# Two layers of a hybrid decoder trunk on one core: q and k blocks set between conv blocks, rotation moved to ScalarE and GpSimd, norm sums and reciprocals moved

## The chip, the cores and the metric

The kernel runs on one core of a Trainium2 chip. The core has TensorE (matmuls, called PE in the profile), VectorE (DVE), ScalarE (ACT), GpSimd (POOL) and SyncE (SP), which here issues the loads. Each engine works through its own queue in program order and waits on semaphores for the others. The metric is the time of one execution in microseconds (us); lower is better.

## What is computed

`reference.py`, cut to the layer (256 tokens, 1024 channels, two layers, 4 retention heads with q and k of 128 and v of 256):

```python
h = rmsnorm(x, norm_mix)
cb, cc, cu, q, k, v, g, ga, gb = split(h @ w_in)
y_conv = (cb * causal_conv3(cc * cu, conv_w)) @ w_conv_out
q, k   = rotary(q, positions) * 128**-0.5, rotary(k, positions)
o      = retention(q, k, v)          # decayed causal scores, then values
o      = (o - mean(o)) * rsqrt(var(o) + eps) * ret_norm     # per head
y_ret  = (silu(g) * o) @ w_ret_out
x = x + (sigmoid(ga) * y_conv + sigmoid(gb) * y_ret) @ w_o
x = x + square(relu(rmsnorm(x, norm_mlp) @ w_up)) @ w_down
# after both layers: rmsnorm(x, norm_final)

def rotary(t):                       # per head, halves of 64
    return concat([t1*cos - t2*sin, t1*sin + t2*cos])
```

## The kernel before

All activations lie with channels on the 128 partitions and the 256 tokens along the row. Every float32 operand of a big matmul is kept as two parts in a reduced float32 form, hi (a rounded copy) and lo (the rest), and three of the four products are taken. `split` (L102) makes the parts: ScalarE casts hi (L103), VectorE subtracts to get lo (L104).

The weights come as 152 blocks of 1 MB, in the order in which they are used: per layer 4 for v (blocks 0 to 3), 28 in the order of `IN_ORDER` (L39), then 4 each for the conv output, the retention output and the output projection, 16 for the MLP up and 16 for down. `window(products)` (L137) handles one block: window i first runs the work booked for it, in between splits both halves of block i+2 (1024 columns each, `parts`), then issues the 32 matmuls of block i, then the load of block i+3, then small products booked for this window. So VectorE splits two blocks ahead of TensorE. There are two buffers for raw weights, three for parts and three for the results of a projection.

Work is booked by hand: `at(n, fn, ph=...)` (L122) puts a step n windows later, at phase -1 or 0 (before the first half's split), 1 (between the halves) or 2 (behind them); `products_at` (L125) books small matmuls. Within a window the steps run in the order in which they were booked, and each engine's queue follows that order. A projection's result is taken in one window later by `collect` (L232): a ScalarE copy of one half and a VectorE add of the other.

In the mixing stage, with windows numbered by their block within the layer:

- The norm's sums over channels are a TensorE product with ones (`norm_total`, L420); in the window after it `factors_begin` (L409) and one more later `factors_end` (L415) make the factors `rr` and `rr2` in twelve VectorE steps. It is booked for window 5 in layer 0 and for window 2 in layer 1. `rotations` (L424, window 10) multiplies the cosine and sine tables by them, q's on VectorE (L425, L426) and k's on GpSimd.
- g takes blocks 4 and 5, conv groups 0 and 1 (cc, cu, cb) 6 to 11, q and k 12 to 15, conv groups 2 and 3 16 to 21, g again 22 and 23, ga 24 to 27, gb 28 to 31.
- `rotate` (L449) takes q or k of two heads: GpSimd multiplies by the cosines (L451), VectorE multiplies the two halves of 64 partitions crosswise by the sines (L453, L454), GpSimd adds (L455); a window later the parts are split.
- The conv (L507 to L530) has GpSimd multiplies at `conv_c`, `conv_u`, `conv_in` and `conv_b`, and four VectorE taps in `conv_in`.
- `scores` (L536) of head h is booked 1 + h windows after block 16; `mix_values` (L549), `gate_values` (L560) and `head_sums` (L571) give per head the values' squares, their split `osq`, and their sums over channels `var_ps`. `head_roots` (L577) makes a square root on ScalarE, a window later a reciprocal on VectorE, two windows later a Newton step (`newton`, L239) and `head_out` (L593), a multiply and a split.

## Time and profile before

| what | before |
|---|---|
| median of 3 runs | 906.25 us (905.71 to 907.66) |
| the profiled execution | 909.5 us, span 907.7 us |
| TensorE busy | 885.3 us, 98% |
| VectorE busy | 709.2 us, 78% |
| ScalarE busy | 512.9 us, 57% |
| GpSimd busy | 258.0 us, 28% |
| granted TensorE clock | 0.998 |

The span runs from the first instruction to the last of the profiled execution; all later rows are of it. The rows of an engine in order of time give start, length, engine, line, operation, result and inputs, shape and count, and in square brackets how long the engine had been idle before and what ended that. Layer 0 reaches to some 458 us, with its mixing stage up to 277, and layer 1 from there on.

### The profile page before, as it was taken

What the parts mean: (1) busy time and instruction counts of PE and PEld (TensorE: products, weight loads), DVE (VectorE), ACT (ScalarE), POOL (GpSimd) and SP (SyncE); (2) the same over time, 40 slices, a digit from 0 to 9 for tenths busy, and PEclk for the clock granted to TensorE, in tenths of its full rate; (3) what the DMA queues carried; (4) which work ended last, traced back from release to release, by engine and by line L of the source; (5) the groups of instructions that cost most, each with busy time, mean ns of one, the idle gap of its engine ahead of it and who ended that gap; (6) DMA issues with size and microseconds to landing.
All of it is one profiled execution on the core that took longest, in us unless ns stands there. A gap on an engine that the chain in (4) does not pass through costs nothing.

```text
span 907.7 us, 12561 instructions
## 1 busy us (share of the span) xinstructions
PE 885.3 (98%) x5026; PEld 764.6 (84%) x5026; DVE 709.2 (78%) x796; ACT 512.9 (57%) x733; POOL 258.0 (28%) x168
## 2 busy tenths in 40 slices
PE   9988999999999999999999999999999999999996
PEld 6867788878888888888888888888888888888896
DVE  5779999999898766555567999999999896664551
ACT  5835455765556777544445543656665577763350
POOL 0646545422112322100010655452211222220110
PEclk9999999999999999999999999999999999999999
DMA  8534454445654555555555444544465455555531
GB/s 285 189 133 170 168 179 164 183 144 182 232 192 180 195 186 186 197 185 187 187 184 193 156 174 152 190 182 142 159 247 181 185 202 186 186 192 185 183 138 46
DMA packets 23818, 163.00 MB, mean 180 GB/s; under 512 B 2768, under 2 KB 3152, under 8 KB 4432
## 3 DMA queue, kind: packets, MB, share of 16 engines
q1 hardware_dynamic: 23184, 161.36, 50.3%
q10 hardware_dynamic: 576, 0.84, 0.3%
q8 instruction: 39, 0.64, 0.3%
q14 instruction: 19, 0.16, 0.0%
HBM read 161.14 MB, written 1.05 MB: 179 GB/s over the span
## 4 chain that ended last, share of the span: by engine, by line
PE 64%; DVE 23%; issue 4%; POOL 3%; DMA 3%; ACT 2%; SPq 0%; DVEq 0%; ACTq 0%; POOLq 0%
PE ps L165 64%; DVE parts L104 14%; DMA raw<-w 3%; DVE sum L236 2%; DVE rot L454 1%; ACT parts L103 1%; DVE acc L518 1%; DVE yc L104 1%; POOL ta L504 0%; POOL red L369 0%; DVE sg L565 0%; DVE sg L498 0%; DVE acc L521 0%; POOL ang L384 0%; DVE sg L236 0%
## 5 line engine op out<-in xcount | busy, mean ns | idle before, releaser
L104 DVE TENSOR_TENSOR parts<-raw,parts 128x1024 fp32r<-128x1024 f32 x305 | 434.4, 1462 | 90.9 <-ACT parts L103 90.2
L103 ACT CAST parts<-raw 128x1024 fp32r<-128x1024 f32 x305 | 305.9, 1050 | 138.1 <-PE ps L165 85.0
L165 PE MATMUL ps<-mix,parts 128*128 128x512 f32 (+1 forms) x1792 | 322.9, 340 | 11.0 <-DVE parts L104 7.5
L165 PEld LDWEIGHTS ps<-mix,parts 128*128 128x128 f32 x1792 | 274.5, 188 | 54.8 <-DVE parts L104 10.0
L165 PE MATMUL ps<-up,parts 128*128 128x512 f32 (+1 forms) x1088 | 182.3, 330 | 0.0
L165 PE MATMUL ps<-mlp,parts 128*128 128x512 f32 (+1 forms) x1024 | 181.6, 340 | 0.0
L165 PEld LDWEIGHTS ps<-up,parts 128*128 128x128 f32 x1088 | 160.6, 189 | 21.1
L165 PEld LDWEIGHTS ps<-mlp,parts 128*128 128x128 f32 x1024 | 157.0, 188 | 23.8
L236 DVE TENSOR_TENSOR sum<-ps,sum 128x512 f32<-128x512 f32 x78 | 53.3, 684 | 45.5 <-ACT sum L235 45.3
L730 POOL TENSOR_TENSOR u<-u,rr2m 128x512 f32<-128x512 f32 x32 | 46.1, 1441 | 131.3 <-ACT u L729 118.3
L235 ACT COPY sum<-ps 128x512 f32<-128x512 f32 x78 | 45.3, 581 | 51.3 <-PE ps L165 51.3
L285 POOL TENSOR_TENSOR mix_sum<-mix_sum,sq 128x512 f32<-128x512 f32 x8 | 12.6, 1574 | 155.7 <-ACT sq L283 155.6
L165 PE MATMUL ps<-yc,parts 128*128 128x512 f32 (+1 forms) x256 | 45.6, 340 | 0.0
L165 PE MATMUL ps<-yr,parts 128*128 128x512 f32 (+1 forms) x256 | 45.5, 340 | 0.0
L165 PE MATMUL ps<-mg,parts 128*128 128x512 f32 (+1 forms) x256 | 45.5, 340 | 0.0
L165 PEld LDWEIGHTS ps<-yr,parts 128*128 128x128 f32 x256 | 39.2, 188 | 6.0
L165 PEld LDWEIGHTS ps<-yc,parts 128*128 128x128 f32 x256 | 39.2, 188 | 6.0
L165 PEld LDWEIGHTS ps<-mg,parts 128*128 128x128 f32 x256 | 39.2, 188 | 6.0
L165 PE MATMUL ps<-parts,mix 128*128 128x512 f32 x180 | 41.8, 392 | 0.0
L165 PEld LDWEIGHTS ps<-parts,mix 128*128 128x128 f32 x180 | 33.6, 188 | 7.4 <-ACT mix L271 0.2
L694 DVE SCALAR_TENSOR_TENSOR px_sb<-ps,px_sb 128x256 f32<-128x256 f32 x60 | 24.0, 421 | 15.6 <-PE ps L165 14.6
L642 POOL TENSOR_TENSOR sum<-sum,rr 128x512 f32<-128x512 f32 x8 | 15.8, 1979 | 59.2 <-DVE sum L236 59.2
(175 smaller groups left out, 668.1 us busy)
## 6 DMA issues: line engine op xcount, KB each, us to landing
raw<-w SPq DMA_DIRECT2D x151, 1024.0 KB, 4.8
raw<-w SPq DMA_DIRECT2D x2, 256.0 KB, 4.4
raw<-w SPq DMA_DIRECT2D x1, 512.0 KB, 5.6
px_sb<-px SPq DMA_DIRECT2D x1, 512.0 KB, 8.3
mask_sb<-mask SPq DMA_DIRECT2D x1, 512.0 KB, 5.7
out<-o SPq DMA_DIRECT2D x2, 256.0 KB, 2.4
out<-o ACTq DMA_DIRECT2D x2, 256.0 KB, 2.4
px_sb<-px SPq DMA_DIRECT2D x1, 256.0 KB, 5.8
```

The source lines that it names most:

```text
L103: nc.scalar.copy(hi, src)
L104: nc.vector.tensor_tensor(out=lo, in0=src, in1=hi.bitcast(F32), op=ALU.subtract)
L165: nc.tensor.matmul(o, lhsT=a, rhs=b, start=start, stop=stop, skip_group_check=True)
L235: nc.scalar.copy(t, ps[:, :, 1, :])
L236: nc.vector.tensor_tensor(out=t, in0=ps[:, :, 0, :], in1=t, op=ALU.add)
L285: nc.gpsimd.tensor_tensor(out=self.sum, in0=self.sum, in1=sq, op=ALU.add)
L454: nc.vector.tensor_tensor(out=w_[64:128], in0=t[0:64], in1=both(sinr[0:64, :]), op=ALU.mult)
L518: nc.vector.scalar_tensor_tensor(out=acc[:, j, 1:], in0=z[:, j, :T - 1], scalar=w1, in1=acc[:, j, 1:], op0=ALU.mult, op1=ALU.add)
L642: nc.gpsimd.tensor_tensor(out=z, in0=z, in1=both(rr2), op=ALU.mult)
L694: nc.vector.scalar_tensor_tensor(out=xk, in0=ps[:, j, half, :], scalar=scale, in1=xk, op0=ALU.mult, op1=ALU.add)
L730: nc.gpsimd.tensor_tensor(out=u, in0=u, in1=both(rr2), op=ALU.mult)
```

## The change

- `IN_ORDER`: of the blocks 9 to 15, q, q, k and k now take 9, 11, 13 and 15, and cc, cu, cb of conv group 1 take 10, 12, 14.
- `rotate`: VectorE's two crosswise multiplies are gone. A window later `rotate_halves` copies the halves crosswise on ScalarE and multiplies the whole by the sines on GpSimd, then adds as before; the split of the parts moves one window on. The sign of the sine table is turned to fit.
- `norm_total` is booked for window 5 in both layers, `rotations` for window 9.
- The reciprocal of the heads comes two windows after the root, between the halves of that window's split; the Newton step and `head_out` come one window later than before, and `head_out`'s multiply moves from VectorE to GpSimd.
- `scores` come one window later; seven small buffers in place of six.

```diff
     [("g", G0), ("g", G0 + 256)]
-    + _conv(0) + _conv(1)
-    + [("q", Q0), ("q", Q0 + 256), ("k", K0), ("k", K0 + 256)]
+    + _conv(0)
+    + [e for qk, c in zip((("q", Q0), ("q", Q0 + 256), ("k", K0)), _conv(1)) for e in (qk, c)]
+    + [("k", K0 + 256)]
     + _conv(2) + _conv(3)
...
-            products_at(5, norm_total)
-        else:
-            products_at(2, norm_total)
-        at(10, rotations)
+        products_at(5, norm_total)
+        at(9, rotations)
...
             nc.gpsimd.tensor_tensor(out=d, in0=t, in1=both(cosr), op=ALU.mult)
-            w_ = t2("rot")
-            nc.vector.tensor_tensor(out=w_[0:64], in0=t[64:128], in1=both(sinr[64:128, :]), op=ALU.mult)
-            nc.vector.tensor_tensor(out=w_[64:128], in0=t[0:64], in1=both(sinr[0:64, :]), op=ALU.mult)
+            at(1, rotate_halves, p, t, sinr)
+
+        def rotate_halves(p, t, sinr):
+            w_, d = t2("rot"), qk[:, 2 * p:2 * p + 2, :]
+            nc.scalar.copy(w_[0:64], t[64:128])
+            nc.scalar.copy(w_[64:128], t[0:64])
+            nc.gpsimd.tensor_tensor(out=w_, in0=w_, in1=both(sinr), op=ALU.mult)
             nc.gpsimd.tensor_tensor(out=d, in0=d, in1=w_, op=ALU.add)
...
-            at(1, lambda: nc.vector.reciprocal(rs, rs))
-            at(2, lambda: newton(rs, t2("rs_a", "rs", 1), rm[:, 1, h, :]))
+            at(2, lambda: nc.vector.reciprocal(rs, rs), ph=1)
+            at(3, lambda: newton(rs, t2("rs_a", "rs", 1), rm[:, 1, h, :]))
             for n in range(2):
-                at(2 + n, head_out, 2 * i + n, rs[:, n, :])
+                at(3 + n, head_out, 2 * i + n, rs[:, n, :])
...
-            nc.vector.tensor_tensor(out=y, in0=y, in1=both(rs), op=ALU.mult)
+            nc.gpsimd.tensor_tensor(out=y, in0=y, in1=both(rs), op=ALU.mult)
             at(1, split, y, *yr.pair(h))
...
-                    products_at(1 + h, scores, h)
+                    products_at(2 + h, scores, h)
...
-    cst[:half, 1], cst[half:, 1] = 2.0, -2.0
+    cst[:half, 1], cst[half:, 1] = -2.0, 2.0
```

The queues show where the steps land. VectorE from the first rotation of layer 0 on, before (`rot` are the crosswise multiplies, `sum` a collect, `parts` the split of a weight block):

```order
L236 TENSOR_TENSOR sum<-ps,sum 128x512
L453 TENSOR_TENSOR rot<-sum,sinq 64x512
L454 TENSOR_TENSOR rot<-sum,sinq 64x512
L104 TENSOR_TENSOR parts<-raw,parts 128x1024 x2
L104 TENSOR_TENSOR q_parts<-qk,q_parts 128x512
L236 TENSOR_TENSOR sum<-ps,sum 128x512
L453 TENSOR_TENSOR rot<-sum,sinq 64x512
```

and now, where the collect of q's second pair is the third `sum`:

```order
L237 TENSOR_TENSOR sum<-ps,sum 128x512
L105 TENSOR_TENSOR parts<-raw,parts 128x1024 x2
L237 TENSOR_TENSOR sum<-ps,sum 128x512
L105 TENSOR_TENSOR parts<-raw,parts 128x1024 x2
L105 TENSOR_TENSOR q_parts<-qk,q_parts 128x512
L237 TENSOR_TENSOR sum<-ps,sum 128x512
```

The multiplies are gone, and a conv block's collect and split stand between two of q.

GpSimd at the same place, before (`qk` is the multiply by the cosines and the final add, `acc` and `sum` are conv steps):

```order
L524 TENSOR_TENSOR acc<-acc,rr 128x512
L529 TENSOR_TENSOR acc<-sum,acc 128x512
L451 TENSOR_TENSOR qk<-sum,cosq 128x512
L455 TENSOR_TENSOR qk<-qk,rot 128x512
L451 TENSOR_TENSOR qk<-sum,cosq 128x512
```

and now:

```order
L527 TENSOR_TENSOR acc<-acc,rr 128x512
L532 TENSOR_TENSOR acc<-sum,acc 128x512
L450 TENSOR_TENSOR qk<-sum,cosq 128x512
L457 TENSOR_TENSOR rot<-rot,sinq 128x512
L458 TENSOR_TENSOR qk<-qk,rot 128x512
L645 TENSOR_TENSOR sum<-sum,rr_138 128x512
L450 TENSOR_TENSOR qk<-sum,cosq 128x512
```

Each rotation has a third GpSimd step, and a conv step follows it.

VectorE at the first pair of heads' reciprocal in layer 0, before (`rm` is the root, `osq` the split of a head's squares, `ta` the collect of ga):

```order
L588 RECIPROCAL rm<-rm 128x512
L565 SCALAR_TENSOR_TENSOR sg<-o_ps,hg,sg 128x256 x2
L236 TENSOR_TENSOR ta<-ps,ta 128x512
L104 TENSOR_TENSOR parts<-raw,parts 128x1024 x2
L241 TENSOR_TENSOR rs_a<-rm 128x512
L242 SCALAR_TENSOR_TENSOR rs_a<-rs_a,rm 128x512
L243 SCALAR_TENSOR_TENSOR rm<-rs_a,rm 128x512
L598 TENSOR_TENSOR sg<-sg,rm 128x512
L104 TENSOR_TENSOR osq<-osq 128x256
```

and now, from the same `sg` step on:

```order
L568 SCALAR_TENSOR_TENSOR sg<-o_ps,hg,sg 128x256 x2
L237 TENSOR_TENSOR ta<-ps,ta 128x512
L105 TENSOR_TENSOR parts<-raw,parts 128x1024 x2
L105 TENSOR_TENSOR osq<-osq 128x256
L237 TENSOR_TENSOR ta<-ps,ta 128x512
L105 TENSOR_TENSOR parts<-raw,parts 128x1024
L591 RECIPROCAL rm<-rm 128x512
L105 TENSOR_TENSOR parts<-raw,parts 128x1024
```

The last `osq` split, which stood behind the reciprocal and the Newton step, now stands ahead of them, and the reciprocal is between two halves of a block's split.

## Rows read from the trace of the kernel before

**Rows 1.** The page's busy time of each engine: us, share of the span, instructions.

```profile
PE 885.3 (98%) x5026; PEld 764.6 (84%) x5026; DVE 709.2 (78%) x796; ACT 512.9 (57%) x733; POOL 258.0 (28%) x168
```

**Rows 2.** Groups of TensorE: count, busy us and mean ns, idle us before and releasers.

```profile
L165 PE MATMUL ps<-mix,parts 128*128 128x512 f32 (+1 forms) x1792 | 322.9, 340 | 11.0 <-DVE parts L104 7.5 <-ACT parts L103 1.2 <-DVE sum L236 1.0
...
L165 PE MATMUL var_ps<-osq,ones 128*128 128x512 f32 x8 | 3.2, 444 | 2.4 <-DVE osq L104 2.4
```

**Rows 3.** TensorE in order of time, layer 0, from block 15 on.

```profile
100.88 5.92 PE L165 MATMUL ps<-mix,parts 128*128 128x256 f32 x32 [0.47 <-DVE parts L104]
107.99 5.92 PE L165 MATMUL ps<-mix,parts 128*128 128x256 f32 x32 [1.20 <-DVE parts L104]
...
121.95 5.59 PE L165 MATMUL ps<-mix,parts 128*128 128x256 f32 x31 [0.44 <-DVE parts L104]
...
192.24 0.50 PE L165 MATMUL var_ps<-osq,ones 128*128 128x512 f32 x1 [1.60 <-DVE osq L104]
```

**Rows 4.** TensorE in order of time, layer 1, from block 4 on.

```profile
480.56 79.29 PE L165 MATMUL ps<-mix,parts 128*128 128x512 f32 x448
...
630.40 0.50 PE L165 MATMUL var_ps<-osq,ones 128*128 128x512 f32 x1 [0.79 <-DVE osq L104]
630.74 17.11 PE L165 MATMUL ps<-mix,parts 128*128 128x512 f32 x96
```

**Rows 5.** VectorE in order of time, layer 1, windows 5 to 18.

```profile
487.97 2.36 DVE L104 TENSOR_TENSOR parts<-raw,parts 128x1024 fp32r<-128x1024 f32 x2 [0.25 <-ACT parts L103]
...
516.54 0.96 DVE L425 TENSOR_TENSOR cosq<-cos_t,rr 128x256 f32<-128x256 f32 x1
...
527.46 0.47 DVE L518 SCALAR_TENSOR_TENSOR acc<-sum,px_sb,acc 128x255 f32<-128x255 f32 x1
...
534.66 0.68 DVE L236 TENSOR_TENSOR sum<-ps,sum 128x512 f32<-128x512 f32 x1
535.37 0.69 DVE L453 TENSOR_TENSOR rot<-sum,sinq 64x512 f32<-64x512 f32 x1
536.07 1.69 DVE L454 TENSOR_TENSOR rot<-sum,sinq 64x512 f32<-64x512 f32 x1
537.79 3.45 DVE L104 TENSOR_TENSOR parts<-raw,parts 128x1024 fp32r<-128x1024 f32 x2
541.17 0.68 DVE L104 TENSOR_TENSOR q_parts<-qk,q_parts 128x512 fp32r<-128x512 f32 x1
541.77 0.68 DVE L236 TENSOR_TENSOR sum<-ps,sum 128x512 f32<-128x512 f32 x1
...
566.56 0.41 DVE L545 TENSOR_TENSOR sc<-sc_ps,mask_sb 128x256 f32<-128x256 f32 x1
```

**Rows 6.** VectorE in order of time, layer 1, windows 6, 7 and 9.

```profile
492.67 0.69 DVE L236 TENSOR_TENSOR sg<-ps,sg 128x512 f32<-128x512 f32 x1 [1.02 <-ACT sg L235]
...
498.33 0.69 DVE L236 TENSOR_TENSOR sum<-ps,sum 128x512 f32<-128x512 f32 x1 [2.35 <-ACT sum L235]
...
512.38 4.24 DVE L104 TENSOR_TENSOR parts<-raw,parts 128x1024 fp32r<-128x1024 f32 x2
```

**Rows 7.** GpSimd in order of time, layer 1: two conv multiplies of one shape.

```profile
499.10 1.31 POOL L642 TENSOR_TENSOR sum<-sum,rr 128x512 f32<-128x512 f32 x1 [33.16 <-DVE sum L236]
...
520.28 2.22 POOL L642 TENSOR_TENSOR sum<-sum,rr 128x512 f32<-128x512 f32 x1 [2.17 <-DVE sum L236]
```

**Rows 8.** VectorE in order of time, layer 1, windows 27 and 28.

```profile
619.24 3.34 DVE L588 RECIPROCAL rm<-rm 128x512 f32<-128x512 f32 x1
...
629.93 0.42 DVE L104 TENSOR_TENSOR osq<-osq 128x256 fp32r<-128x256 f32 x1
...
630.87 3.46 DVE L104 TENSOR_TENSOR parts<-raw,parts 128x1024 fp32r<-128x1024 f32 x2
```

**Rows 9.** VectorE in order of time, layer 0, window 9.

```profile
69.69 1.12 DVE L498 SCALAR_TENSOR_TENSOR sg<-th,sg 128x512 f32<-128x512 f32 x1 [2.21 <-ACT th L497]
```

**Rows 10.** ScalarE in order of time, layer 1: a collect's copy.

```profile
540.72 0.58 ACT L235 COPY sum<-ps 128x512 f32<-128x512 f32 x1
```

More of the change, by code (lines that the diff above doesn't have):

```diff
@@ L75, in trunk_kernel @@
     ones_f = const.tile([P, 1], F32, name="ones_f")
-    idle = tmp.tile([P, 2 * T], BF16, tag="tmp1", bufs=6, name="idle")
+    idle = tmp.tile([P, 2 * T], BF16, tag="tmp1", bufs=7, name="idle")
     cst_sb = const.tile([P, 2], F32, name="cst_sb")
@@ L291, in split_sum @@
         def split_sum(self):
-            self.sums = tuple(tmp.tile([P, T], F32R, tag="tmp1", bufs=6, name=f"{self.name}_{n}") for n in ("sh", "sl"))
+            self.sums = tuple(tmp.tile([P, T], F32R, tag="tmp1", bufs=7, name=f"{self.name}_{n}") for n in ("sh", "sl"))
             split(self.sum[:, 0, :], *self.sums)
@@ L327, in trunk_kernel @@
     nc.scalar.activation(eps2, eps, AF.Square)
-    xs = tmp.tile([P, T], F32, tag="tmp1", bufs=6, name="xs")
+    xs = tmp.tile([P, T], F32, tag="tmp1", bufs=7, name="xs")
     nc.vector.tensor_scalar(out=xs, in0=x[:, 0, :], scalar1=norm.gain[:, 0:1], scalar2=None, op0=ALU.mult)
@@ L362, in late_loads @@
     def late_loads():
-        pos_i = tab["pos"] = tmp.tile([P, T], I32, tag="tmp1", bufs=6, name="pos_i")
+        pos_i = tab["pos"] = tmp.tile([P, T], I32, tag="tmp1", bufs=7, name="pos_i")
         nc.sync.dma_start(out=cst_sb, in_=cst)
@@ L371, in reduce_angles @@
     def reduce_angles():
-        ang, turns, red = (tmp.tile([P, T], F32, tag="tmp1", bufs=6, name=nm) for nm in ("ang", "turns", "red"))
+        ang, turns, red = (tmp.tile([P, T], F32, tag="tmp1", bufs=7, name=nm) for nm in ("ang", "turns", "red"))
         tab.update(ang=ang, turns=turns)
@@ L386, in sines @@
     def sines():
-        half_sin = tab["sh"] = tmp.tile([P, T], F32, tag="tmp1", bufs=6, name="sh")
+        half_sin = tab["sh"] = tmp.tile([P, T], F32, tag="tmp1", bufs=7, name="sh")
         ang, turns = tab["ang"], tab["turns"]
@@ L409, in factors_begin @@
         def factors_begin(norm=norm):
-            rs_m, rs_a = (tmp.tile([P, T], F32, tag="tmp1", bufs=6, name=n) for n in ("rs_m", "rs_a"))
+            rs_m, rs_a = (tmp.tile([P, T], F32, tag="tmp1", bufs=7, name=n) for n in ("rs_m", "rs_a"))
             rsqrt_begin(rr, rs_m, norm.total_ps, 1.0 / D)
@@ L786, in square_last @@
         def square_last(k, ps):
-            sq = tmp.tile([P, T], F32, tag="tmp1", bufs=6, name="sq1")
+            sq = tmp.tile([P, T], F32, tag="tmp1", bufs=7, name="sq1")
             nc.scalar.activation(sq, ps, AF.Square)
```

## The prediction

> **What bounds the kernel now.** I read the page's busy times first, then the groups of TensorE, then each engine in order of time. TensorE is busy for 885.3 of 907.7 us [rows 1], and the change adds no matmul, so all that can be won is idle time of TensorE. The groups put nearly all of it in two places: 11.0 us ahead of the projections on the normed input ("ps<-mix,parts") and 2.4 us ahead of the head sums ("var_ps") [rows 2]. The chain of waits runs through VectorE for most of both mixing stages; that only says that VectorE is there as late as TensorE, and what counts is where TensorE really stood still.
>
> In order of time, layer 1 shows none in its first blocks: fourteen blocks in 79.29 us, 5.66 us a block [rows 4]; that is the floor. In layer 0 TensorE waits for the lo half of a block at 100.88, 107.99, 115.11 (the same length as 107.99) and 121.95: 0.47 + 1.20 + 1.20 + 0.44 = 3.31 us [rows 3]. These are the blocks that VectorE splits while it takes in q, q, k, k. The head sums wait 1.60 us in layer 0 and 0.79 in layer 1 [rows 3, 4]. The other 7.7 us of the 11.0 lie before these, at the start of layer 0.
>
> Why q and k are slow is in the VectorE rows [rows 5]: from one collect to the next 7.11 us (534.66 to 541.77), 1.45 over the floor, four times in a row. The two half multiplies take 0.69 and 1.69 us for the same shape, and the two splits 3.45 us where the plain pair takes 2.36. The second multiply and the splits run while GpSimd runs, and GpSimd's own multiply takes 1.31 us alone but 2.22 beside VectorE [rows 7]. So a GpSimd multiply isn't free to VectorE: it costs it 1.00 to 1.09 us. That decides this change, since it moves work from VectorE to GpSimd.
>
> **The change part by part.** I number the windows of a layer by their block. Rows that follow each other overlap by some 0.08 us, so I count from start to start: split pair 2.28, a 128x512 step 0.60, a 128x256 one 0.34, the four conv taps 1.83, a half multiply 0.70 [rows 5, 8].
>
> *The price of GpSimd.* Windows 10 to 17 of layer 1 take VectorE from 516.54 to 566.56, 50.0 us or 6.25 a window [rows 5]. The VectorE work alone is 8 x 2.28 + 8 x 0.60 + four rotations of 1.5 + 1.83 + two table steps 0.84 + five 128x512 steps 3.0 + two short ones 0.66 = 35.4. GpSimd has 13 full multiplies and two half ones there, 14 in all: (50.0 - 35.4)/14 = 1.05 us each.
>
> *Rotation and order.* Per rotation VectorE loses 1.4 us of multiplies, and gains one more GpSimd multiply, 1.05: only 0.35 us is saved. What the order does is more: the four long windows are apart. VectorE's own work in windows 10 to 17 after the change is 8 x 2.28 + 8 x 0.60 + 1.83 + five steps 3.0 + one short 0.33 = 28.2, and GpSimd has 17 multiplies, 17.9: 46.1 us, 5.76 a window. One by one: 5.1, 6.0, 4.5, 6.0, 7.4, 6.0, 4.9, 6.0. Against 5.66 the lateness runs -0.5, -0.2, -1.3, -0.9, +0.8, +1.2, +0.4, +0.8. If VectorE enters window 10 with no lead, as in layer 0, TensorE stands 1.2 us in place of 3.3: **2.1 us won in layer 0**. The ScalarE copies of 64 rows are two of at most 0.58 us [rows 10], on an engine with 57% busy, behind the cast of a block that isn't due yet: nothing, unless that queue is held (second rival). The changed sign of the sine table costs nothing.
>
> *Factors a window earlier.* The q factors move ahead of window 9's gate step. In layer 0 VectorE is idle there for 2.21 us [rows 9], in which the two could run (0.96 each beside GpSimd [rows 5]); but the gate step waits for a GpSimd multiply that they would slow, so between 1.8 us won and 1 us lost; I take zero, since the multiplies queued on GpSimd there are what the idle waits for.
>
> *Reciprocals.* Before, the 3.34 us reciprocal, the Newton step and a 128x512 multiply stand on VectorE ahead of the split of the last squares ("osq", 629.93), for which the head sums wait [rows 8]. Now the split of the squares comes ahead of the reciprocal, sooner by more than its 3.34 us and so by more than the 1.60 that TensorE waited, and what ends last there is TensorE's own earlier block: **2.4 us won in both layers**. The reciprocal now stands between the halves of a block's split. The next to be late is that second half, but VectorE works there ahead: the split from 630.87 ends at 634.3 [rows 8], and its block starts one block after 630.74 [rows 4], at 636.4, and needs the second half at some 639. That hides 3.3 us; with the cover gone it would be up to 3.3 us for each of four.
>
> *Head outputs to GpSimd.* Eight multiplies of 0.60 leave VectorE and eight of 1.05 on it come: 0.45 x 8 = 3.6 us more for VectorE, four of them a layer. The windows behind (the conv output projection) have only two 128x512 steps and a split, 3.5 us, so it is caught up there: zero.
>
> *Norm sums later in layer 1.* Twelve steps of 128x256 (0.42 each [rows 8], 5.1 us in all) leave windows 3 and 4 for 6 and 7. The first waits for TensorE's column sums behind block 5, which ends at 480.56 + 2 x 5.66 = 491.9, while VectorE has been free since 487.97 + 2.36 = 490.3 [rows 4, 5]: some 2 us, with the value steps and the gate's collect queued behind. It fills idle times of 1.02 and 2.35 us [rows 6] and three of 0.25, 4.1 in all, and the factors (2 x 0.96) come a window sooner. 2.0 + 5.1 - 4.1 + 1.9 is 4.9; some of it lies where the splits ran beside GpSimd, and I take 4.4 us for the start of window 9's split, at 512.38 [rows 6]. Its block is due at 480.56 + 7 x 5.66 = 520.2, and the first half was ready at 514.5: 5.7 us of cover, 1.3 left or, with the heavier GpSimd traffic, about 1.1. The peak of 1.2 then gives **0.1 us lost**.
>
> The sum: 2.1 + 2.4 - 0.1 = 4.4 us. The profiled execution took 909.5 us (span 907.7 and 1.8 around it), which gives 905.1; from the median of 906.25 it is **901.9 us**.
>
> **The rivals.** *GpSimd costs VectorE its whole length (slower).* If each multiply holds VectorE for the 1.31 us that it takes alone [rows 7], 34 multiplies in the two stretches add 0.26 each, 8.8 us: 906.25 - 4.4 + 8.8 = 910.7. It decides from 1.18 us a multiply (no change). For it: each rotation has three in a row now, and layer 1 has no lead left. Against it: two in one window cost (4.24 - 2.36)/2 = 0.94 [rows 6], less than one alone.
>
> The Trainium skill, "SBUF — State Buffer", section "Who interferes with whom", speaks for this rival: a VectorE step with two SBUF inputs and a GpSimd step that reads SBUF share a port, and the one that comes second is blocked until the first has finished. By that rule alone the price is the full 1.31 and the time this rival's; the rows agree that the two exclude each other, but show 1.05 us of the 1.31, and by them the sum stands.
>
> *ScalarE held by GpSimd (same).* ScalarE's q cast, the conv scaling and the yc cast now stand behind GpSimd chains of three, 3 x 2.22 = 6.7 us against a window of 5.66. If windows 14 and 16 each lose 0.75 us in both layers, 3 us come back: 904.9. Against it: two windows together bring GpSimd 8.9 us of 11.3.
>
> *The factors fall into the idle time (faster still).* At 0.94 a multiply the peak of 1.2 goes, 5.7 us won, and with the 1.8 of the factors 7.5: 898.8.
>
> *The wait at the head sums stays*, because the squares' GpSimd sum or its cast is what comes last: 2.4 back, 904.3. In the rows the split starts where the multiply before it ends, so VectorE's order is what held it.
>
> **How the numbers follow.** Forecast 0.55 (900.5, at 0.94 a multiply, to 904.4); factors in the idle time 0.13; head sums stay 0.04; ScalarE held 0.17; GpSimd's whole length 0.11. About 0.2%, 1.8 us, is what a measurement can tell here: faster means under 904.4. Faster 0.55 + 0.13 + 0.04 = 0.72; same 0.17; slower 0.11. The range runs from 898.8 (the best rival) to 907.0 (a price a little over 1.18), with some 0.05 below and 0.12 above.
>
> **What would show it.** Waits of TensorE: the four at q and k at most 1.5 us in sum, "var_ps" none, layer 1 under 0.5 before its head sums. VectorE: windows 10 to 17 in 46 us, split pairs of 3.4 to 4.4, reciprocals between two splits. GpSimd: eight more multiplies at the rotation at 2.2 us, eight at the head outputs. I am wrong if layer 1 shows TensorE waiting for splits between 515 and 560 us, if the split pair beside three multiplies grows past 4.5, or if ScalarE's casts show waits for GpSimd that end after VectorE asks for them.

## The result, and the profile after

| what | before | after |
|---|---|---|
| median | 906.04 us (905.71 to 907.66, 4 runs) | 891.07 us (890.09 to 892.57, 4 runs) |
| ratio, 95% interval | | 0.9833 (0.9814 to 0.9851) |
| the profiled execution | 909.5 us, span 907.7 | 891.4 us, span 889.6 |
| TensorE busy, 5026 matmuls each | 885.3 us | 873.4 us |
| waits ahead of "ps<-mix,parts" and "var_ps" | 11.0 + 2.4 us | 6.7 + 0 us |

Faster, as forecast, but by 15 us where 4.4 were forecast, and outside the range. The page's busy line of after:

```profile
PE 873.4 (98%) x5026; PEld 762.5 (86%) x5026; DVE 705.1 (79%) x772; ACT 524.1 (59%) x749; POOL 294.2 (33%) x184
```

The groups of TensorE in after (count, busy us and mean ns of one, idle us before them and what ended it), beside [rows 2]:

```profile
L166 PE MATMUL ps<-mix,parts 128*128 128x512 f32 (+1 forms) x1792 | 320.5, 339 | 6.7 <-DVE parts L105 3.1 <-DVE sum L237 2.1 <-ACT vt L471 1.5
L166 PE MATMUL ps<-up,parts 128*128 128x512 f32 (+1 forms) x1088 | 179.3, 326 | 0.0
L166 PE MATMUL ps<-mlp,parts 128*128 128x512 f32 (+1 forms) x1024 | 178.4, 336 | 0.0
...
L166 PE MATMUL var_ps<-osq,ones 128*128 128x512 f32 x8 | 2.7, 420 | 0.0
```

and two groups of before that the prediction had not looked at, since nothing waits there:

```profile
L165 PE MATMUL ps<-up,parts 128*128 128x512 f32 (+1 forms) x1088 | 182.3, 330 | 0.0
L165 PE MATMUL ps<-mlp,parts 128*128 128x512 f32 (+1 forms) x1024 | 181.6, 340 | 0.0
```

The span is 18.1 us shorter. Waits of TensorE account for 4.3 + 2.4 = 6.7 us of it. The other 11 to 12 us are TensorE's own busy time: the same matmuls of the same shapes, in stages that the change does not touch and in which TensorE waits for nothing, are 4 ns each shorter. That is the part to be explained.

**The waits.** TensorE in after in order of time (start, length, operation and count; in brackets the idle time ahead and what ended it), both layers:

```profile
35.37 5.92 PE L166 MATMUL ps<-mix,parts 128*128 128x512 f32 x32 [1.51 <-ACT vt L471]
...
60.39 11.14 PE L166 MATMUL ps<-mix,parts 128*128 128x256 f32 x63 [1.72 <-DVE parts L105]
73.67 0.47 PE L166 MATMUL ps<-mix,parts 128*128 128x512 f32 x1 [2.14 <-DVE sum L237]
75.47 46.16 PE L166 MATMUL ps<-mix,parts 128*128 128x256 f32 x255 [1.34 <-DVE parts L105]
...
184.91 0.64 PE L166 MATMUL var_ps<-osq,ones 128*128 128x512 f32 x2
...
479.98 72.42 PE L166 MATMUL ps<-mix,parts 128*128 128x512 f32 x416
...
616.10 0.64 PE L166 MATMUL var_ps<-osq,ones 128*128 128x512 f32 x2
```

From 75.47 on 255 matmuls follow each other with no wait: the four waits at q and k of [rows 3] are gone, and in layer 1 thirteen blocks pass with none, so moving the norm sums and putting more on GpSimd took nothing there. Both second head sums come without the waits of [rows 3, 4]. What is left, 1.51 + 1.72 + 2.14 + 1.34 = 6.7 us, lies in the first twelve blocks of layer 0.

VectorE in after, layer 1: the first and the last row of windows 10 to 17 with the two longest waits between them, the first step of the norm factors, and the second reciprocal's window:

```profile
480.18 0.42 DVE L248 TENSOR_SCALAR rs_m<-mix_st 128x256 f32<-128x256 f32 x1 [1.96 <-PE mix_st L166]
...
508.05 0.68 DVE L501 SCALAR_TENSOR_TENSOR sg<-th,sg 128x512 f32<-128x512 f32 x1
...
525.27 4.09 DVE L105 TENSOR_TENSOR parts<-raw,parts 128x1024 fp32r<-128x1024 f32 x2 [1.16 <-ACT parts L104]
...
542.89 0.69 DVE L105 TENSOR_TENSOR yc<-acc,yc 128x512 fp32r<-128x512 f32 x1 [0.40 <-ACT yc L104]
...
552.22 1.51 DVE L105 TENSOR_TENSOR k_parts<-qk,k_parts 128x256 fp32r<-128x256 f32 x1
...
610.85 0.41 DVE L105 TENSOR_TENSOR osq<-osq 128x256 fp32r<-128x256 f32 x1
...
614.36 3.34 DVE L591 RECIPROCAL rm<-rm 128x512 f32<-128x512 f32 x1
```

From 508.05 to the step that opens window 18, at 552.22, are 44.2 us, 5.52 a window, where 50.0 were in [rows 5] and 46.1 were forecast; 1.9 of them are idle. The last squares are split at 610.85, ahead of the reciprocal at 614.36, and TensorE wants them at 616.10.

**The pace.** The first fourteen blocks behind the norm of the MLP in layer 0, before:

```profile
288.90 79.31 PE L165 MATMUL ps<-mlp,parts 128*128 128x512 f32 x448
```

and after:

```profile
280.25 77.82 PE L166 MATMUL ps<-mlp,parts 128*128 128x512 f32 x448
```

5.66 us a block against 5.56, with no wait in either. The busy time in stretches of 60 us (busy of TensorE with its matmuls, granted clock, DMA share, GB/s), before:

```profile
300.00:360.00 60.00, 60.00 (x342) 1.00 0.54 193
```

and after:

```profile
290.00:350.00 60.00, 60.00 (x349) 1.00 0.57 204
```

The granted clock is 1.00, its 2.4 GHz level, in both; yet TensorE starts 2% more matmuls. The starts of single matmuls show how. In such a stretch a matmul of 512 columns and one of 256 alternate; the distances between starts, in ns, read from the two traces at 320 us, are:

```
before: 120 236 113 233 117 241 | 120 236 113 233 117 241     6 matmuls in 1060 ns, 5.65 us a block of 32
after:  117 230 116 230 117 230 | 116 230 117 230 116 230     6 matmuls in 1040 ns, 5.55 us a block of 32
```

(The second also comes as 113 232 118 231 112 233, in the same 1040 ns.) These are two paces, not a spread: every long stretch of every trace here holds the one or the other until something comes between. That can be little: twice a stretch changed where a single start was 4 ns out of place. I call the two paces slow and fast. Counted over windows of 12 matmuls, before's profile has 3775 matmuls in the slow pace and 342 in the fast one, after's 600 and 3521: some 3180 matmuls at 3.3 ns, 10.5 of the 11.9 us.

### The profile page after: what moved, and what is told of

Its sections match the earlier page's. It is cut to its first block, busy times and chain, and to the rows that moved or that the text cites. A ratio compares the mean times of both kernels' runs of the same rounds, so it can differ in the third digit from the quotient of the medians.

```text
span 889.6 us, 12565 instructions
## 1 busy us (share of the span) xinstructions
PE 873.4 (98%) x5026; PEld 762.5 (86%) x5026; DVE 705.1 (79%) x772; ACT 524.1 (59%) x749; POOL 294.2 (33%) x184
## 3 DMA queue, kind: packets, MB, share of 16 engines
HBM read 161.14 MB, written 1.05 MB: 182 GB/s over the span
## 4 chain that ended last, share of the span: by engine, by line
PE 71%; DVE 17%; DMA 4%; POOL 3%; issue 2%; ACT 2%; SPq 0%; DVEq 0%; ACTq 0%; POOLq 0%
PE ps L166 70%; DVE parts L105 10%; DMA raw<-w 4%; ACT parts L104 1%; DVE sum L237 1%; DVE rm L591 1%; PE o_ps L166 1%; POOL rot L457 1%; POOL qk L450 1%; POOL ta L507 1%; POOL qk L458 0%; DVE acc L521 0%; DVE acc L524 0%; DVE rs_a L242 0%; DVE rs_a L243 0%
## 5 line engine op out<-in xcount | busy, mean ns | idle before, releaser
L166 PE MATMUL ps<-up,parts 128*128 128x512 f32 (+1 forms) x1088 | 179.3, 326 | 0.0
L166 PE MATMUL ps<-mlp,parts 128*128 128x512 f32 (+1 forms) x1024 | 178.4, 336 | 0.0
```

Of the source, the lines that this page charges most:

```text
L166: nc.tensor.matmul(o, lhsT=a, rhs=b, start=start, stop=stop, skip_group_check=True)
```

## The experiments

Two questions: what sets the pace, and which part of the change brings what. The theory was that the phase in which the stream of matmuls is broken and restarts decides (A); the rival, that the pace follows from load elsewhere (VectorE, GpSimd, loads) or from the parts of the change directly (B). Each kernel was timed against the kernel before on its own chip; a ratio has its 95% interval. "Fast" and "slow" with a count are matmuls in the two paces in its profile.

**Reciprocals alone.** The kernel before, with

```diff
-            at(1, lambda: nc.vector.reciprocal(rs, rs))
-            at(2, lambda: newton(rs, t2("rs_a", "rs", 1), rm[:, 1, h, :]))
+            at(2, lambda: nc.vector.reciprocal(rs, rs), ph=1)
+            at(3, lambda: newton(rs, t2("rs_a", "rs", 1), rm[:, 1, h, :]))
...
-                at(2 + n, head_out, 2 * i + n, rs[:, n, :])
+                at(3 + n, head_out, 2 * i + n, rs[:, n, :])
```

> The kernel before with the reciprocals' part of the change alone. Theory A (TensorE's pace is set anew at each restart of its matmul stream and then kept; the change won 11.9 us of its time by that, above all because the head sums no longer wait): the 2.4 us of wait at var_ps go, and behind the second head sums the matmuls come at 173.3 ns on average in place of 176.6, for some 1400 matmuls in layer 0 and 1300 in layer 1: 4.6 + 4.3 + 2.4 = 11 us, about 895. Theory B (the pace belongs to the new block order, the moved rotation or the buffers): 2.4 us, about 903.6, and 176.6 ns throughout.

Measured: 901.33 us against 909.4, ratio 0.9928 (0.9904 to 0.9951). The wait at "var_ps" is 0. Behind the second head sums of both layers the pace is fast for 364 matmuls. It ends at the output projection ("mg"), in layer 1 behind a wait of 0.34 us and in layer 0 behind two starts that come 0.19 us late together; layer 0 then runs slow to its end: 1732 fast, 2357 slow. More than the 2.4 us of the wait, less than if the fast pace had held.

**The change without the reciprocals.** The kernel after, with those lines turned back.

> The changed kernel with the reciprocals where they were before (the head outputs stay on GpSimd). Theory A: waits at var_ps of 1 to 2.4 us come back, and behind them the slow pace of 176.6 ns: 891 + 2 + 9 = about 902. Theory B: the pace stays at 173.3 ns, about 893.

Measured: 895.43 us against 909.4, 0.986 (0.9841 to 0.9879). "var_ps" waits 1.1 us, the pace behind it stays fast for only 117 matmuls and is then mostly slow up to the output projection, in layer 0 up to the MLP, but the MLP of both layers runs fast (3132 fast, 959 slow). So the reciprocals are one way to the fast pace, and not the only one.

**Seven buffers alone.** The kernel before, with `bufs=7` in place of 6 for the small tiles.

> The kernel before with seven small buffers in place of six and nothing else, so that the tiles behind them lie elsewhere in memory. Theory A: no difference, 906.0 within 0.2%, pace 176.6 ns from 193 us on. Theory B in its form that the place of the buffers sets the pace: 173.3 ns and about 894.

Measured: 904.42 us against 909.4, 0.9958 (0.9942 to 0.9974), where no difference was expected. "var_ps" waits 2.0 us, and the pace is mostly slow (1150 fast, 2953 slow), but 822 matmuls of the MLP in layer 1 are fast. The buffer does more than it seems. The rows of VectorE and TensorE in before, early in layer 0:

```profile
49.15 0.43 DVE L241 TENSOR_TENSOR rs_a<-rr 128x256 f32<-128x256 f32 x1 [4.22 <-POOL ang L384]
...
52.56 0.46 PE L165 MATMUL ps<-mix,parts 128*128 128x512 f32 x1 [0.77 <-DVE sg L236]
53.60 5.60 PE L165 MATMUL ps<-mix,parts 128*128 128x256 f32 x31 [0.58 <-DVE parts L104]
60.35 0.49 PE L165 MATMUL ps<-mix,parts 128*128 128x512 f32 x1 [1.16 <-ACT parts L103]
62.57 11.14 PE L165 MATMUL ps<-mix,parts 128*128 128x256 f32 x63 [1.72 <-DVE parts L104]
```

and with seven buffers:

```profile
45.00 0.87 DVE L241 TENSOR_TENSOR rs_a<-rr 128x256 f32<-128x256 f32 x1
...
40.53 17.41 PE L165 MATMUL ps<-mix,parts 128*128 128x512 f32 x97
59.67 11.34 PE L165 MATMUL ps<-mix,parts 128*128 128x256 f32 x63 [1.73 <-DVE parts L104]
```

With six buffers a step of the norm factors waits 4.22 us for GpSimd's work on another small tile, and TensorE then waits 0.77 + 0.58 + 1.16 = 2.5 us for what comes late behind that step; with seven none of this happens, and the block of 62.57 starts 2.9 us sooner. The three waits of TensorE stand in all ten profiles with six buffers and in none of the ten with seven, the changed kernel's among them. The ratio gives 3.8 us; the rest is within what the pace moves between executions.

**A pair of small matmuls that does nothing.** This changes nothing but the place of a break. The kernel before, and behind block 46, 47 or 48 of each layer (early in the MLP), or behind 46 and 47, the column sums of the norm are formed once more: two matmuls of 256 columns into a tile that nobody reads. The norm's own sums behind block 45 are such a pair too.

```diff
+        def idle_pair(norm=norm):
+            o = ps_misc.tile([P, T], F32, tag="misc", name="idle_ps")
+            column_sums(o, *norm.sums)
+
+        products_at(2, idle_pair)          # 2, 3, 4: behind block 46, 47, 48
```

> The kernel before with two more matmuls of 128x256 behind block 46 of each layer (the second MLP block after the norm's sums; ones by operands that are long there, nothing reads the result), which wait for nothing. Theory A, with the phase read from the traces: in the slow pace the starts lie 233, 117, 241, 120, 236, 113 ns apart, over and over, and two small matmuls put in after ...233, 117 or ...241, 120 were followed by the fast pace, after ...236, 113 by the slow one. Block 46 ends after 233, 117: the pace turns to 173.3 ns for some 920 matmuls in layer 0 and 790 in layer 1, 5.7 us won for 0.5 us of added work: about 900.8. Theory B: the 0.5 us are lost, 906.5, and the pace stays.

> As before, but behind block 47, which ends after ...241, 120 ns where the stream is slow. Theory A: that phase was followed by the fast pace, so 173.3 ns for some 890 and 760 matmuls, 5.5 us won less 0.5: ratio 0.9945. Theory B (the pace belongs to the order or the buffers): ratio 1.0005.

> As the kernel with two more matmuls behind block 46, but behind block 48. Theory A (pace set by the phase at which the stream is broken): where the stream before is slow, block 48 ends after ...236, 113 ns, the phase that kept the slow pace in both layers of the kernel before: 176.6 ns stays behind the pair, and 0.5 us are lost, ratio 1.0005. Theory C (any two matmuls put in, wherever, turn the pace): as behind block 46, ratio 0.995.

> The kernel before with the idle pair behind block 46 of each layer, for a second profile. In the first one the norm sums behind block 45 had already turned the slow stream fast, and the pair came into a fast stream. Phase theory (A), now stated by the last distance between starts ahead of the break: behind 235 or 236 ns a slow stream stays slow, behind 232 or 233 and behind 240 or 241 it turns fast, and a fast stream stays fast. So wherever the norm sums (288 us and 723 us) leave the stream slow, block 46 is slow, the pair comes 16 big matmuls later, behind 233, and the 919 and 790 matmuls behind it are fast. Load theory (B): slow on both sides of the pair. Time 903 to 905 us by A, 905 to 910 by B.

> The kernel before with idle pairs behind block 46 and behind block 47. A: a slow stream turns at the first pair at the latest (at the second one if the phase there should be wrong), and a fast one passes both unchanged, so the MLP of both layers is fast in every execution: about 904.4 us as with one pair, 0.2 us more for the second pair in each layer, spread 3 us. B: as the kernel before, 907 us plus 0.9 for the four pairs, spread 7 us.

Measured:

| idle pair behind block | median us | before us | ratio (95%) |
|---|---|---|---|
| 46 | 904.14 (903.33 to 904.58) | 909.4 | 0.9952 (0.9934 to 0.997) |
| 46, second profile | 903.83, one run | 906.97 | |
| 47 | 904.43 (902.67 to 905.05) | 907.22 | 0.9959 (0.9937 to 0.9982) |
| 48 | 909.46 | 907.22 | 1.0011 (0.9989 to 1.0033) |
| 46 and 47 | 904.87 (903.31 to 907.85) | 906.97 | 0.9978 (0.996 to 0.9995) |

One useless pair behind block 46 or 47 makes the kernel 0.4 to 0.5% faster, and 11 runs with it spread over 2.4 us where before's own spread over 7; behind block 48 it does nothing. Both pairs together bring no more than one, and spread over 4.5 us where 3 were expected. The first profile with the pair behind block 46 could not show why: there the norm's sums behind block 45 had just turned the stream fast in both layers, and the pair came into a fast stream. The second profile shows it in layer 1, TensorE in order of time:

```profile
723.57 0.28 PE L165 MATMUL mlp_st<-mlp_sh,ones 128*128 128x256 f32 x1
723.68 0.28 PE L165 MATMUL mlp_st<-mlp_sl,ones 128*128 128x256 f32 x1
723.80 5.81 PE L165 MATMUL ps<-mlp,parts 128*128 128x512 f32 x32
729.45 0.28 PE L165 MATMUL idle_ps<-mlp_sh,ones 128*128 128x256 f32 x1
```

Block 46 takes 729.45 - 723.80 = 5.65 us, the slow pace; behind the pair 790 matmuls follow at the fast one, as expected. Its busy time in stretches ahead of the pair and behind it:

```profile
660.00:720.00 60.00, 59.73 (x342) 1.00 0.58 207
740.00:800.00 60.00, 60.00 (x348) 1.00 0.55 193
```

and with the pair behind block 48:

```profile
660.00:720.00 60.00, 60.00 (x341) 1.00 0.58 211
740.00:800.00 60.00, 60.00 (x342) 1.00 0.53 191
```

The same loads, the same work on all other engines, the same granted clock: rival B falls for the MLP. The pairs behind 46 and 47 turned a slow stream in three places of the profiles, and left it slow in none; the pair behind 48 met two slow streams and left both slow.

The starts give the rule. In the slow pace the distance behind a 512-column matmul runs 233, 241, 236 and again. Over the profiles of all these kernels, wherever two small matmuls come into a running stream (the norms' sums and the idle pairs), what follows goes by the last such distance:

```
last distance ahead of the break     slow stream goes on slow   slow stream goes on fast
235 or 236 ns                                             21                          0
232 or 233 ns                                              0                         19
240 or 241 ns                                              0                         12
(a fast stream goes on fast in 32 of 32)
```

A block has 16 such matmuls, one more than a multiple of three, so each block moves the break on by one place in the cycle: that is why a slow stream that the norm's sums behind block 45 left slow turns behind 46 and behind 47, and not behind 48. What in the chip makes the two paces no run shows.

**The order alone, the rotation alone.** The kernel before with the new `IN_ORDER` and nothing else (the scores stay where they were, unlike what its expectation says), and the kernel before with the new `rotate`:

```diff
-            w_ = t2("rot")
-            nc.vector.tensor_tensor(out=w_[0:64], in0=t[64:128], in1=both(sinr[64:128, :]), op=ALU.mult)
-            nc.vector.tensor_tensor(out=w_[64:128], in0=t[0:64], in1=both(sinr[0:64, :]), op=ALU.mult)
+            at(1, rotate_halves, p, t, sinr)
...
-                    products_at(1 + h, scores, h)
+                    products_at(2 + h, scores, h)
```

> The kernel before with the new order of the blocks alone (q, q, k and k between conv blocks, scores a window later); the rotation stays on VectorE. VectorE has the same work in windows 10 to 17, 50.0 us less 0.9 of score steps that move on. If it is VectorE's sum that makes TensorE wait (my forecast's reading), the waits at q and k stay at 2 to 3.3 us and the time within 1 us; if it is the four long windows in a row, they fall under 1 us. The pace behind the stretch is not changed by either on its own account: the head sums still wait, so mostly slow; where a run starts anew in the other phase, up to 4 us come off.

> The kernel before with the rotation moved to ScalarE and GpSimd and nothing else (scores a window later, as they need it). At my forecast's price of 1.05 us a GpSimd multiply VectorE saves 0.35 us a rotation, 1.4 a layer: the waits at q and k fall from 3.3 to 1.9 us. At the price that the changed kernel's windows 10 to 17 show, (44.2 - 28.2 - 1.9 of waits)/17 = 0.83, it saves 0.6 a rotation, 2.4 a layer: waits of 0.9 us. Ratio 0.997 to 0.9985, and the slow pace stays.

Measured: the order alone 907.75 us against 907.22, 0.9998 (0.9983 to 1.0014); the rotation alone 902.72 against 907.22, 0.9927 (0.9899 to 0.9954), more than was expected of it. With the order alone the group of TensorE waits as before:

```profile
L166 PE MATMUL ps<-mix,parts 128*128 128x512 f32 (+1 forms) x1792 | 324.5, 342 | 10.9 <-DVE parts L105 8.0 <-ACT parts L104 1.1 <-ACT vt L469 0.8
```

and in order of time the waits have only come together:

```profile
85.62 22.87 PE L166 MATMUL ps<-mix,parts 128*128 128x256 f32 x128 [3.09 <-DVE parts L105]
110.32 12.71 PE L166 MATMUL ps<-mix,parts 128*128 128x256 f32 x63 [1.83 <-DVE parts L105]
```

With the rotation alone:

```profile
L165 PE MATMUL ps<-mix,parts 128*128 128x512 f32 (+1 forms) x1792 | 321.0, 339 | 7.4 <-DVE parts L104 4.2 <-ACT parts L103 1.1 <-DVE sum L236 1.1
...
L165 PE MATMUL ps<-mg,parts 128*128 128x512 f32 (+1 forms) x256 | 46.2, 340 | 1.8 <-DVE mg L685 1.4 <-DVE mg L104 0.4
...
L165 PE MATMUL var_ps<-osq,ones 128*128 128x512 f32 x8 | 3.2, 444 | 3.0 <-DVE osq L104 3.0
```

All 7.4 us lie at the start of layer 0, and behind the last of these waits TensorE runs on past q and k:

```profile
83.54 39.00 PE L165 MATMUL ps<-mix,parts 128*128 128x256 f32 x223 [0.57 <-DVE parts L104]
```

The waits at q and k go with the multiplies, not with the order. The wait at the head sums grows to 3.0 us, and one of 1.8 appears at the output projection: TensorE arrives earlier at places where the next thing is late. The three groups together wait 12.2 us, where before's two profiles have 13.4 and 12.8, so alone the rotation mostly moves its waits on, and most of the 0.7% is pace (2941 fast, 1148 slow in this profile). Only with the new reciprocals do the waits at the head sums go as well.

**The change with one part undone.** The kernel after once more, unchanged, and with one part turned back at a time: the head outputs on VectorE, the norm sums of layer 1 at window 2, the rotation on VectorE, the old order, the factors at window 10.

```diff
+            nc.vector.tensor_tensor(out=y, in0=y, in1=both(rs), op=ALU.mult)      # head outputs
...
+        products_at(5 if layer == 0 else 2, norm_total)                           # norm sums
...
+            nc.vector.tensor_tensor(out=w_[0:64], in0=t[64:128], in1=both(sinr[64:128, :]), op=ALU.mult)   # rotation
+            nc.vector.tensor_tensor(out=w_[64:128], in0=t[0:64], in1=both(sinr[0:64, :]), op=ALU.mult)
...
+    + _conv(0) + _conv(1)                                                         # order
+    + [("q", Q0), ("q", Q0 + 256), ("k", K0), ("k", K0 + 256)]
...
+        at(10, rotations)                                                         # factors
```

> The changed kernel, unaltered, beside the three that undo one part of it. Both theories: ratio 0.983 again. Theory A adds: the fast pace of 173.3 ns in the same places (behind the second head sums of both layers and behind the norm's sums), some 3500 of 4200 matmuls.

> The changed kernel with the multiply of the head outputs back on VectorE. My forecast put this part at zero: no wait of TensorE goes or comes, so within 1 us of the changed kernel. Only a small wait elsewhere that breaks the stream in another phase could move it, by up to 3 us a stretch.

> The changed kernel with layer 1's norm sums in window 2 again. My forecast put the move at 0.1 us lost for waits of VectorE. Theory A: in the changed kernel these sums, behind block 5, turned the pace from slow to fast for 375 matmuls; behind block 2 they come before the stream has its 512, 256 beat, so blocks 4 to 17 of layer 1 stay at 176.6 ns, 1.3 to 1.5 us lost: ratio to the changed kernel 1.0015.

> The changed kernel with the rotation's multiplies back on VectorE (order, reciprocals, head outputs, norm sums and factors as changed). By the run with the order alone, VectorE's sum makes TensorE wait: 2 to 3.5 us of waits come back in layer 0 and, with the norm sums' work ahead of them, up to 3 in layer 1; behind the head sums the pace is fast as in the changed kernel: 894 to 898, ratio 0.987 to 0.991.

> The changed kernel with the blocks in the order before (q, q, k, k behind conv group 1), all else as changed. If the order carries the gain at q and k, as my forecast had it, the four long windows in a row are back and 2 us or more of waits with them: ratio 0.983 or more. If the order is idle, as the run with the order alone suggests, the waits stay at 5 to 7 us and the ratio at 0.980.

> The changed kernel with the rotation factors in window 10, as before. My forecast put their move at zero for TensorE. In the changed kernel VectorE spends 3.0 us on two of them in layer 0 before the gate step, while GpSimd has the same port busy, and TensorE then waits 2.1 us for the collect behind and 1.3 for a split: if the factors are what is late, 1 to 2 us of that go, ratio 0.979; if they only fill the wait for the gate's tanh, nothing changes.

| the kernel after, with | median us | ratio to before (95%) | wait at "ps<-mix,parts" | fast, slow |
|---|---|---|---|---|
| nothing undone | 891.2 | 0.9802 (0.9781 to 0.9824) | 5.0 | 2628, 1496 |
| head outputs on VectorE | 890.72 | 0.982 (0.9771 to 0.9868) | 5.7 | 3679, 492 |
| norm sums at window 2 | 892.4 | 0.9818 (0.98 to 0.9837) | 5.2 | 3017, 1121 |
| rotation on VectorE | 898.72 | 0.9887 (0.9867 to 0.9907) | 10.0 | 3316, 759 |
| old order | 892.26 | 0.9819 (0.9788 to 0.9849) | 4.4 | 2285, 1854 |
| factors at window 10 | 891.29 | 0.9822 (0.9791 to 0.9852) | 6.5 | 2396, 1711 |

The first four rows come from one chip, the last two from another (before's medians there: 909.24 and 906.71 us). Unaltered, the kernel gave the same time again, but its fast pace fell short of the 3500 matmuls expected: in this profile the MLP of layer 1 ran slow. In this table the rotation is the only part whose undoing costs something outside the intervals, 7.5 us, and in the profiles 5.0 of waits come back. The reciprocals, turned back further above, gave 0.986, above both ratios of the unaltered kernel (0.9802 and 0.9833). The seventh buffer was not undone by itself. The group of TensorE in that kernel:

```profile
L166 PE MATMUL ps<-mix,parts 128*128 128x512 f32 (+1 forms) x1792 | 324.5, 341 | 10.0 <-DVE parts L105 8.7 <-ACT vt L467 0.6 <-DVE sum L237 0.6
```

The norm sums at window 2 bring 468 slow matmuls in layer 1's mixing stage, which all other versions of this table begin fast; at 3.3 ns that is 1.5 us, and 1.2 were measured, which the intervals do not tell from none. No version is clearly better than the kernel after.

**The kernel before once more, unchanged.**

> The kernel before, unaltered, beside the two: whether its waits of 13 us and its slow pace behind the head sums come again, and how far its times spread. Theory A: waits at both second head sums, and behind each a pace that may be the slow or the fast one, so spreads of 3 to 5 us between executions, where the changed kernel, which does not wait there, spreads less.

Measured: 907.76 us (903.21 to 909.35, 10 runs) against 906.71, 1.0007 (0.9983 to 1.0031). Its profiled execution was the shortest, 903.21 us, with a span of 901.4. The page's busy line of it:

```profile
PE 879.7 (98%) x5026; PEld 761.9 (85%) x5026; DVE 708.9 (79%) x796; ACT 512.6 (57%) x733; POOL 258.9 (29%) x168
```

and the same fourteen blocks:

```profile
288.96 77.81 PE L165 MATMUL ps<-mlp,parts 128*128 128x512 f32 x448
```

The same program, 5.56 us a block here and 5.66 in the profile that the prediction was made from; 2229 fast, 1863 slow. Its waits are nearly the same, 10.4 us and 1.9 at "var_ps". So the pace differs between executions of one kernel: before's spread over 902 to 911 us, and the profile shown was one that ran slow nearly throughout. After's lie at 890 to 894.

**Why after runs fast more often.** In the profile of before that the prediction used, the second head sums are the last place in each mixing stage at which TensorE waits. Over the profiles of all these kernels, the pace behind them was fast in 18 of 18 stretches where they come without a wait (the new reciprocals; 9 profiles, two layers), and in 12 of 22 where TensorE waits for them. In all 40 stretches the stream ahead of these sums is slow and its last distance 232 or 233 ns, the place from which the small matmuls of the table turned a slow stream fast in 19 of 19. So a break without a wait falls well there each time, as the table would have it, though the head sums have 512 columns and the pairs 256. A wait differs in length from run to run and seems to leave the phase to chance; the 12 of 22 fit that, and no run set the length of the wait by itself.

**The pace set on purpose in the changed kernel.** The kernel after, with idle pairs behind blocks 46 and 47 of each layer.

> The kernel after with idle pairs behind blocks 46 and 47 of each layer. A: the MLP of both layers is fast in every execution. The kernel after had 822 slow matmuls of layer 1's MLP in one profile of two, 2.7 us; the four pairs cost 0.9 us. So 891.2 less 0 to 1.8 where it was slow, plus 0.9 where it was fast: 890 to 892 us, with a smaller spread, ratio 0.980 to 0.983. No slow stretch behind block 46. B: 892.1, and slow MLP stretches remain.

Measured: 892.69 us (891.67 to 893.68) against 906.97, 0.984 (0.9816 to 0.9865). The MLP of both layers is fast, as expected, but its streams were fast ahead of the pairs already, and the kernel is not better than after's 891.1 and 891.2 us (ratios 0.9833 and 0.9802), and just above the time expected.

## Why the prediction was wrong in size

**The step that failed** is the first: "all that can be won is idle time of TensorE", with 5.66 us a block as "the floor". The number was read from one stretch of one execution, and that stretch was in the slower of two paces. Of the 18.1 us between the two profiles, 11.9 are busy time. Between the second profile of each kernel (903.21 and 893.64 us) it is 879.7 - 877.6 = 2.1. By the medians, 15 us less some 7 of waits (11.0 + 2.4 - 6.7 = 6.7 between the first profiles, 10.4 + 1.9 - 5.0 = 7.3 between the second), the pace is worth some 8 us to this change, by this estimate. The forecast and its range were built from waits alone and left that term out.

**A part put at nothing without a reason** is the seventh small buffer: the prediction has no term for it. It took 0.77 + 0.58 + 1.16 = 2.5 us of waits off the start of layer 0, where before's 7.7 us of waits became 6.7 in one profile of after and 4.0 in the other; the first of these has two longer waits, 1.51 and 2.14 us, where before has 0.52 and 0.73, and why is open. Without the buffer the waits won between the first profiles come to 3.3 + 2.4 - 1.5 = 4.2 us, at q and k, at the head sums and at the start; that this is near the 4.4 forecast is in part luck.

**Waits at q and k: the mechanism was right, the cause within it half wrong.** Forecast 1.2 us left of 3.3; in after's first profile none is left, in its second 0.29 + 0.74 = 1.03. But I wrote "What the order does is more", and the runs say the opposite: the order alone leaves 10.9 us of waits, the change without it has 4.4. The lateness at the end of the stretch is a sum over all eight windows, and setting long windows apart does not change the sum; taking work out of four of them does.

**The price of a GpSimd multiply was mis-sized**: forecast 1.05 us of VectorE's time. Of the 44.2 us, 28.2 are the work that the prediction counted and 1.9 idle, which leaves (44.2 - 28.2 - 1.9)/17 = 0.83. Most of GpSimd's multiplies still take 2.2 to 2.3 us there, as in [rows 7]. With 0.83 for the added multiply a rotation saves VectorE 0.57 us and not 0.35. The two GpSimd steps that it had before came down with it, so that by the same averages the whole rotation costs VectorE 1.4 + 2 x 1.05 - 3 x 0.83 = 1.0 us less, 4.0 for the four: enough for the 3.3 us of waits, all of which the rotation alone took away where 0.9 to 1.9 were expected to stay. This is an estimate, from averages over mixed steps. The rival that GpSimd costs its whole 1.31 us falls with this; so does the rule of the Trainium skill, "SBUF — State Buffer", section "Who interferes with whom", taken as a price for each step: 17 multiplies at 1.31 would have made the stretch 52.4 us with the idle time.

**Head sums: right.** 2.4 us of waits forecast gone, 2.4 gone, and the second half of the split next to the reciprocal was not late. Its second effect, on the pace, was not foreseen.

**Norm sums: right in the wait, wrong in the sign of the rest.** VectorE waits 1.96 us for the sums at 480.18, where 2.0 were forecast, and TensorE does not notice. The 0.1 us of loss did not come; what the move does is to let layer 1's mixing stage start in the fast pace (375 to 468 matmuls, 1.2 to 1.5 us).

**Head outputs and factors: right**, nothing each as far as intervals of some 4 and 3 us to either side can tell: 890.72 and 891.29 with them undone against 891.2.

**ScalarE held by GpSimd: fell.** ScalarE in after, layer 1:

```profile
524.18 2.00 ACT L104 CAST parts<-raw 128x1024 fp32r<-128x1024 f32 x2 [2.15 <-DMA raw<-w]
...
540.01 0.41 ACT L104 CAST k_parts<-qk 128x256 fp32r<-128x256 f32 x1 [3.82 <-POOL qk L458]
...
542.24 0.62 ACT L104 CAST yc<-acc 128x512 fp32r<-128x512 f32 x1 [1.82 <-POOL acc L532]
```

Its casts do wait for GpSimd, 3.82 us for the k parts and 1.82 for yc, and VectorE waits 0.40 us for the second: the sign of being wrong shows, at a size that TensorE does not feel. VectorE's longer wait, 1.16 us at 525.27, is for a cast that had itself waited for a weight load.

## What to carry to other kernels

Before a block time is called a floor, read it in several stretches and in a second profile of the same kernel; here two readings of one program differed by 2% with the same granted clock and no wait. A wait removed from the bounding engine is worth its own length plus what the restart behind it does; an experiment that changes nothing but the restart, such as the idle pair, separates the two. Where an engine falls behind over several windows, count its total work there: rearranging it moves the wait, only taking work away shortens it. And every line of the change wants a term, the number of buffers too: here the seventh was worth 2.5 us, more than the order, the norm sums, the factors and the head outputs are shown to be.

## What the runs showed of the hardware

- A stream of matmuls of 512 and 256 columns in turn has two stable paces at the same granted clock, 1040 and 1060 ns for six. A pace holds until something comes between (951 matmuls in a row), and two small matmuls turn the slow one into the fast one at two places of three in its cycle.
- A multiply on GpSimd (1.31 us alone, 2.2 to 2.3 beside VectorE) cost VectorE 0.83 to 1.05 us on average in two mixes of the same steps, an estimate from what VectorE's own work leaves of the stretch.
- Behind the waits of 2.14 and 1.34 us in layer 0 after had a stretch at the lower of the clock's levels, 1.2 GHz, and then the upper one again. Its busy time in stretches (TensorE, weight loads, VectorE, ScalarE, GpSimd, then granted clock, DMA share, GB/s):

```profile
76.00:79.30 3.30, 3.30 (x12) 2.79 (x11) 3.30 (x4) 2.72 (x4) 0.55 (x1) 0.51 0.24 50
80.00:90.00 10.00, 10.00 (x60) 8.74 (x59) 9.94 (x8) 6.87 (x10) 8.69 (x5) 1.00 0.63 220
```

Twelve matmuls in 3.3 us where the fast pace has nineteen: some 1.2 us lost once. Before had no such stretch there.
